# Bidirectional HGRN2 scan beside dense products: where the second key transposes land, how the diagonal score blocks are placed, and how the filler is dealt out at the scan's two ends

## The chip, the core and the metric

The kernel runs on one core of one Trainium2 chip. The metric is the device time of one execution in microseconds (us). TensorE (PE), VectorE (DVE), ScalarE (ACT), GpSimd (POOL) and SyncE (SP) each take their own list of instructions in order and wait for each other by semaphores. PSUM, where TensorE writes, has eight banks of 128 x 512 float32.

## What is computed

One layer of an encoder over 1024 positions of width 1024, in float32. The part around the change is a gated linear recurrence with eight heads of 128, run forwards and backwards, over the projections of the normalised input (shortened):

```python
def _chunk_gated_scan(q, k, v, lf):        # S_t = diag(f_t) S_{t-1} + k_t v_t^T,  o_t = S_t^T q_t
    a = jnp.cumsum(lfb, axis=2)
    decay = jnp.where(tril, jnp.exp(jnp.minimum(a_t - a_s, 0.0)), 0.0)
    scores = jnp.einsum("bhtk,bhsk,bhtsk->bhts", qb, kb, decay)
    o = einsum("bhts,bhsv->bhtv", scores, vb) + einsum("bhtk,bhkv->bhtv", qb * jnp.exp(a), state)
    new_state = jnp.exp(a_last)[..., None] * state + einsum("bhsk,bhsv->bhkv", kb * jnp.exp(a_last - a), vb)

def _token_mixers(h, w_in, ...):
    proj = jnp.einsum("bsd,de->bse", h, w_in)      # conv input, q, v, two forget gates, output gate, two merge gates
    o = _bi_hgrn2(q, v, z_f, z_b, lb[0], lb[1])    # one scan per direction, added
    bmix = rmsnorm_per_head(o) * norm_w * silu(og)
    return sigmoid(g_a) * (a @ pw_w) + sigmoid(g_b) * (bmix @ o_w)
```

Behind it stand an output product, a gated feed-forward block with a short convolution, and a last RMSNorm.

## The kernel before

**Stages.** The kernel projects the normalised input in tiles of 128 columns (first one by one, then in pairs with seven products in place of eight), runs the convolution branch, then the scan, then the products with hgrn_o_w and w_out, then the feed-forward block. The positions are split into two halves of 512. Large products write each float32 operand as a high and a low part and take three matmuls for one (`mm3`, lines 139 to 149: L147, L148 and L149 of the profile).

**The scan** (lines 1026 to 1405) goes over eight heads and, within a head, two halves of 512 positions: sixteen iterations, numbered i = 0 to 15 below. An odd i is a second half. For each one it

- loads q, v and the two gates' inputs (`scan_inputs`, L1067, L1070, L116) and makes the gates on ScalarE (L1071 to L1073);
- builds keys and queries by doubling (`scan_base`, `double_keys`, `double_queries`, L1052), with ScalarE copies of them in another order (L974), and takes score blocks of a width of 32 from them (`level`, L1103), collected in the tile D on VectorE by `copy_predicated` (L1167, L1204);
- takes the wider blocks of 32 and 64 into one bank (`blocks`, L1186), which ScalarE copies to the score tile S (L1214); four more ScalarE copies then place the four diagonal blocks of D into S, one for each group of 32 partitions (L1216);
- turns the keys of both directions with four transposes each (`scan_states`, L1226), which ScalarE copies to kT (L1228), and multiplies them with v for the states (L1235).

One head later `outputs` and `scan_outputs` chain the backward states (L1328), form the outputs from S, v and the states in the one bank of the tag "ob" (L1276), normalise them (L1278, L1281, L510, L511, L1295), turn them back (L1302) and store them gated (L1304, L1308).

**The banks** are dealt out by tag: three "mm", two "sc", two "tr", one "ob" (L97). The dense products accumulate in "mm" banks. Both key transposes, v's transposes (L1376) and the outputs' transposes take "tr" banks.

**The order.** TensorE's list is the program's own order; the lists of the other engines come from a scheduler. What keeps TensorE busy in the scan is `dense`, a stream of 176 pieces of dense products: the last 18 tiles of the input projection, eight pieces each, and the convolution's 1024 columns, four pieces for each of eight tiles. A piece is six matmuls. `Stream.fill(n)` adds n to a debt and executes whole pieces while the debt is at least 1. An iteration has five steps, and after each, `between(FILL)` calls dense.fill(1.82), then one step of the next iteration's base (`ahead.step`), then one step of the previous head's outputs (`pending.fill(1)`). The wait for a score block of 32 stands behind an iteration's first step, that for 64 behind its second.

At the scan's beginning 6 pieces go ahead of the first base, and 3 behind each of its five steps. At its end (lines 1387 to 1401) the last head's outputs are done in steps with pieces in between: `left - 20` comes out negative there, so the debt eats the next pieces, and two are executed ahead of `bm_loads(0)`, eight behind it. `bm_loads` brings the finished heads back for the product with hgrn_o_w, which follows.

A DMA may be issued from SP, from ACT (`nc.scalar.dma_start`) or from POOL; before, ACT issues none. In the built program the DMAs of SP and ACT share eight semaphores in turn, and each waits until the one that had its semaphore last, the eighth before it, has landed.

## Time and profile before

| what | value |
|---|---|
| median of 3 runs | 1783.46 us (1782.06 to 1784.79) |
| the profiled execution | 1786.31 us |
| its span, first to last instruction | 1784.5 us |
| granted TensorE clock, mean | 0.994 |
| the scan with its two ends in the span | about 497 to 917 us |

In a row of the timeline stand the start, the length, the engine, the line, what is written and read, and in brackets the idle time ahead of it with the instruction that ended it. In a row of the waits stand the total, the count and the longest. A row of the windows has the length, then the busy time of each engine with its instructions in brackets, the granted clock, the DMA engines' share and GB/s. A row of the groups ends with busy time, mean ns of one, and the idle time ahead. SPq is SP issuing DMAs.

### The profile page before, as it was taken

The page shows a single profiled execution, that of the slowest core. Times are in us where ns is not written, and L with a number is a line of the kernel's source. Part 1 is how long each engine was busy: PE and PEld are TensorE (multiplying, and loading weights), DVE is VectorE, ACT ScalarE, POOL GpSimd, SP SyncE. Part 2 cuts the span into 40 slices and gives each one's busy share as a digit, 9 for nine tenths or more (in the row PEclk, how much of TensorE's full clock was granted, in tenths as well). Part 3 has the DMA queues.
Part 4 walks back from the last instruction along what each step waited for, and adds up shares of the span by engine and source line. Part 5 has one row for each costly group of instructions (what it writes and reads, how often), then busy time and mean ns, then how long its engine had stood idle before and what let it go on. Part 6 is the DMA issues. An engine that isn't in the chain of part 4 may idle for free.

```text
span 1784.5 us, 30262 instructions
## 1 busy us (share of the span) xinstructions
PE 1733.0 (97%) x11878; PEld 1424.5 (80%) x11878; DVE 1213.2 (68%) x1845; ACT 827.8 (46%) x1582; POOL 152.1 (9%) x165
## 2 busy tenths in 40 slices
PE   8989999999999999999999999999999999999997
PEld 6878877788778888777878887778888888888885
DVE  5599999746678788877446567667667667544455
ACT  7344333234467778776551244344344344422123
POOL 2201111000000000000000002011111111000000
PEclk9999999999999999999999999999999999999998
DMA  8758877756653434435367665667767666534233
GB/s 283 218 151 189 190 179 185 181 162 206 196 183 102 126 120 126 131 103 178 120 216 226 195 201 177 159 146 156 154 143 153 147 147 138 159 103 125 78 91 136
DMA packets 321269, 284.46 MB, mean 159 GB/s; under 512 B 14942, under 2 KB 242022, under 8 KB 321126
## 3 DMA queue, kind: packets, MB, share of 16 engines
q1 hardware_dynamic: 279958, 250.01, 44.9%
q0 software_dynamic: 41168, 32.51, 13.0%
q8 instruction: 93, 1.52, 0.4%
q14 instruction: 50, 0.41, 0.1%
HBM read 189.40 MB, written 76.81 MB: 149 GB/s over the span
## 4 chain that ended last, share of the span: by engine, by line
PE 72%; DMA 10%; DVE 9%; issue 4%; ACT 3%; POOL 1%; SPq 0%; POOLq 0%; ACTq 0%; DVEq 0%
PE mm L147 17%; PE mm L148 17%; PE mm L149 17%; PE sc L147 3%; PE sc L149 3%; PE sc L148 3%; DMA sw<-in_w_in_dram 3%; DVE acc L956 2%; PE ob L1276 2%; DMA wr<-in_w_in_dram 2%; DMA wr<-wr 2%; DVE wp L123 2%; PE tr L147 1%; PE tr L148 1%; PE tr L149 1%
## 5 line engine op out<-in xcount | busy, mean ns | idle before, releaser
L147 PE MATMUL mm<-hx,wp 128*128 128x512 f32 x1144 | 458.5, 401 | 12.5 <-DVE ev L718 7.6
L149 PE MATMUL mm<-hx,wp 128*128 128x512 f32 x1144 | 448.5, 392 | 1.9 <-DVE wp L123 1.9
L148 PE MATMUL mm<-hx,wp 128*128 128x512 f32 x1144 | 447.9, 391 | 0.0
L123 ACT CAST wp<-wr 128x1024 fp32r<-128x1024 f32 (+2 forms) x171 | 162.1, 949 | 339.6 <-PE mm L148 241.9
L147 PEld LDWEIGHTS mm<-hx,wp 128*128 128x128 f32 x1144 | 216.1, 189 | 60.1 <-DVE ev L718 10.6
L149 PEld LDWEIGHTS mm<-hx,wp 128*128 128x128 f32 x1144 | 215.8, 189 | 49.4 <-DVE wp L123 3.2
L148 PEld LDWEIGHTS mm<-hx,wp 128*128 128x128 f32 x1144 | 216.3, 189 | 41.9 <-issue 0.2
L123 DVE TENSOR_TENSOR wp<-wr,wp 128x1024 fp32r<-128x1024 f32 (+2 forms) x169 | 187.0, 1107 | 86.1 <-ACT wp L123 85.5
L956 DVE SCALAR_TENSOR_TENSOR acc<-gl,v_b,acc 128x1024 f32<-128x1024 f32 x120 | 149.5, 1284 | 0.4
L1635 DVE TENSOR_TENSOR xr<-mm,xr 128x512 f32<-128x512 f32 x48 | 33.2, 691 | 72.1 <-PE mm L149 72.1
L367 ACT COPY su<-mm 128x512 f32<-128x512 f32 x82 | 47.5, 579 | 69.2 <-PE mm L149 68.1
L123 ACT CAST wq<-sw 128x1024 fp32r<-128x1024 f32 x41 | 43.0, 1050 | 65.5 <-issue 25.9
L1052 DVE TENSOR_TENSOR kG<-kG,tb 128x512 f32<-128x512 f32 x96 | 65.9, 688 | 5.5 <-PE sc L1186 5.5
L1052 DVE TENSOR_TENSOR qF<-qF,tb 128x512 f32<-128x512 f32 x96 | 65.6, 687 | 4.7 <-ACT A L1084 3.4
L1484 DVE SCALAR_TENSOR_TENSOR tm<-gp,v_a,tm 128x512 f32<-128x512 f32 x88 | 66.0, 750 | 2.0
L147 PE MATMUL mm<-hy,wp 128*128 128x512 f32 x164 | 64.7, 395 | 1.6 <-ACT su L367 1.6
L147 PE MATMUL sc<-hy,wq 128*128 128x512 f32 x164 | 64.6, 394 | 0.0
L148 PE MATMUL mm<-hy,wp 128*128 128x512 f32 x164 | 64.3, 392 | 0.0
L149 PE MATMUL sc<-hy,wq 128*128 128x512 f32 x164 | 64.2, 391 | 0.0
L147 PE MATMUL tr<-hx,wp 128*128 128x512 f32 x164 | 63.9, 390 | 0.0
L149 PE MATMUL tr<-hx,wp 128*128 128x512 f32 x164 | 63.8, 389 | 0.0
L148 PE MATMUL tr<-hx,wp 128*128 128x512 f32 x164 | 63.8, 389 | 0.0
(354 smaller groups left out, 3437.2 us busy)
## 6 DMA issues: line engine op xcount, KB each, us to landing
wr<-in_w_in_dram SPq DMA_DIRECT2D x56, 512.0 KB, 5.0
wr<-in_ffn_w_up_dram SPq DMA_DIRECT2D x24, 512.0 KB, 5.5
sw<-in_ffn_w_up_dram SPq DMA_DIRECT2D x44, 256.0 KB, 4.1
d_g<-ft SPq DMA_DIRECT2D x44, 256.0 KB, 2.5
sw<-in_ffn_w_up_dram POOLq DMA_DIRECT2D x20, 512.0 KB, 8.6
sw<-in_w_in_dram SPq DMA_DIRECT2D x38, 256.0 KB, 3.6
d_z<-ev SPq DMA_DIRECT2D x32, 256.0 KB, 4.6
zi<-d_z SPq DMA_DIRECT2D x32, 256.0 KB, 2.6
```

The lines of the kernel that those rows point to most:

```text
L123: parts = A.copy(hi, src), eng.tensor_tensor(lo, src, hi.bitcast(F32), op=ALU.subtract)
L147: T.matmul(acc, whi[:, k, :], ahi, start=first, stop=False, skip_group_check=again)
L148: T.matmul(acc, whi[:, k, :], alo, start=False, stop=False, skip_group_check=again)
L149: T.matmul(acc, wlo[:, k, :], ahi, start=False, stop=last, skip_group_check=again)
L367: A.copy(t, acc)
L956: V.scalar_tensor_tensor(acc, g[:, k : k + S], tap(k), acc, op0=ALU.mult, op1=ALU.add)
L1052: V.tensor_tensor(o, a, b, op=op)
L1276: T.matmul(o[:, sl], l, r, start=(n == 0), stop=(n == len(terms) - 1))
L1484: V.scalar_tensor_tensor(c, g[:, o + k : o + k + H], vec("fdw", k * NF + j), c, op0=ALU.mult, op1=ALU.add,)
L1635: V.tensor_tensor(xr[i][half], acc, xr[i][half], op=ALU.add)
```

## The change

Three edits. The second direction's key transposes go to a "mm" bank, in the rotation of the dense products. The four ScalarE copies that place the diagonal blocks become four DMAs from D to S issued by ScalarE. The filler is dealt out anew: 7 pieces ahead of the first base and 3, 4, 4, 3, 0 behind its steps (21 as before), 1.77 in place of 1.82 after each step of the scan, and at the end a table of output steps and pieces, with the debt set to zero first.

```diff
-FILL = 1.82
+FILL = 1.77
+TAIL = ((1, 2), (1, 1), (2, 4), (2, 3))
...
         A.copy(S_t, c4(b))
         for g in range(0, P, 32):
-            A.copy(S_t[g : g + 32, :, g : g + 32], D_t[g : g + 32])
+            nc.scalar.dma_start(S_t[g : g + 32, :, g : g + 32], D_t[g : g + 32])
...
-            b = bank("tr")
+            b = bank("mm" if d else "tr")
             for c in range(4):
                 T.transpose(b[:, c * P : (c + 1) * P], kG[:, d, c * P : (c + 1) * P], ident)
...
-    dense.fill(6)
-    for _ in range(5):
+    dense.fill(7)
+    for pieces in (3, 4, 4, 3, 0):
         cur.step(1)
-        dense.fill(3)
+        dense.fill(pieces)
...
-    left = 8 * len(rest) + 4 * ND - dense.count
-    pending.fill(1)
-    dense.fill(left - 20)
-    pending.fill(1)
-    dense.fill(4)
-    pending.fill(2)
-    dense.fill(4)
-    pending.fill(2)
-    dense.fill(4)
+    dense.owed = 0
+    for steps, pieces in TAIL:
+        pending.fill(steps)
+        dense.fill(pieces)
     bm_loads(0)
     pending.fill(1)
-    dense.fill(8)
     dense.drain()
     bm_loads(1)
     pending.drain()
```

## The prediction

> **What bounds the kernel now.** First the page: the span, the busy shares, and the chain that ended last.

> ```profile
> span 1784.5 us, 30262 instructions
> ...
> PE 1733.0 (97%) x11878; PEld 1424.5 (80%) x11878; DVE 1213.2 (68%) x1845; ACT 827.8 (46%) x1582; POOL 152.1 (9%) x165
> ...
> PE 72%; DMA 10%; DVE 9%; issue 4%; ACT 3%; POOL 1%; SPq 0%; POOLq 0%; ACTq 0%; DVEq 0%
> ```

> TensorE is busy for 1733.0 of 1784.5 us and the change takes no matmul away, so it can only win idle time. I read next the windows around the scan: its beginning, its body, its end, two stretches of the end alone, a stretch of dense products, and one of VectorE's fullest.

> ```profile
> 497.60:517.00 19.40, 17.47 (x199) 14.22 (x198) 12.56 (x23) 15.61 (x27) 0.00 (x0) 1.00 0.80 256
> 517.00:886.60 369.60, 358.83 (x5676) 300.20 (x5677) 283.76 (x622) 264.61 (x616) 13.11 (x14) 1.00 0.39 125
> 886.60:916.80 30.20, 26.96 (x143) 22.32 (x141) 10.60 (x20) 17.13 (x45) 1.83 (x2) 0.94 0.47 156
> 900.90:904.30 3.40, 1.47 (x6) 0.93 (x7) 0.88 (x2) 2.41 (x8) 0.96 (x1) 1.00 0.00 0
> 904.30:907.70 3.40, 3.40 (x10) 2.64 (x9) 1.95 (x3) 2.07 (x5) 0.00 (x0) 0.50 0.86 274
> 480.00:500.00 20.00, 20.00 (x90) 16.57 (x89) 7.27 (x10) 6.85 (x10) 0.00 (x0) 1.00 0.56 171
> 729.00:760.00 31.00, 28.66 (x495) 23.53 (x495) 28.19 (x59) 23.13 (x47) 0.00 (x0) 1.00 0.45 137
> ```

> TensorE's idle time is 19.40 - 17.47 = 1.93 us at the beginning, 10.77 in the body, 3.24 at the end. After the end's idle stretch (busy 1.47 of 3.40 us) the granted clock is 0.50 for 3.40 us: half of that, 1.7 us, is lost too. All that can be won is thus 1.9 + 10.8 + 3.2 + 1.7 = 17.6 us. A piece of dense products is six matmuls at 20.00 / 90 us, 1.33 us.

> The waits of TensorE from 500 to 925 us name the places:

> ```profile
> PE sc L1186 <- DVE qF L1052: 4.2, 4, 1.8
> PE tr L1226 <- DVE ev L1304: 3.9, 3, 2.0
> PE tr L1226 <- ACT kT L1228: 2.7, 4, 0.7
> PE tr L1302 <- ACT tm L1295: 2.6, 2, 2.1
> PE sc L1103 <- ACT A L1084: 1.9, 2, 1.6
> PE ob L1276 <- ACT tm L1278: 0.7, 1, 0.7
> ```

> They add up to 16.0 us, the idle time above. The timeline places the first kinds (the longer ones; the four waits for the first transposes' copy are 0.67 each, in the second halves of heads 1, 2, 3 and 5, and 3.9 - 2.05 - 1.45 = 0.4 is left for head 7):

> ```profile
> 599.69 0.69 PE L1186 MATMUL sc<-qF,kG 128*64 128x64 f32 x16 [0.88 <-DVE qF L1052]
> 606.31 0.66 PE L1226 MATMUL tr<-ident,kG 128*128 128x128 f32 x4 [0.68 <-ACT kT L1228]
> 744.84 0.66 PE L1226 MATMUL tr<-ident,kG 128*128 128x128 f32 x4 [2.05 <-DVE ev L1304]
> 755.54 0.46 PE L1186 MATMUL sc<-qF,kG 128*32 128x32 f32 x32 [0.29 <-DVE qF L1052]
> 781.73 0.46 PE L1186 MATMUL sc<-qF,kG 128*32 128x32 f32 x32 [1.83 <-DVE qF L1052]
> 832.44 0.69 PE L1186 MATMUL sc<-qF,kG 128*64 128x64 f32 x16 [1.15 <-DVE qF L1052]
> 839.84 0.66 PE L1226 MATMUL tr<-ident,kG 128*128 128x128 f32 x4 [1.45 <-DVE ev L1304]
> ```

> **The change part by part.**

> **Second key transposes in a "mm" bank.** Every wait at L1226 is for a "tr" bank, held by the first transposes' copy or by an output evacuation. In the changed program these transposes carry no wait but that for their own keys, except in the last iteration, where it is for an eviction long done. All 3.9 + 2.7 = 6.6 us go. The price: a dense half comes round to a bank one turn sooner. A half lasts four pieces, 5.3 us, and its eviction by ScalarE is one copy (L1228, of the same size: 588 ns, below), so I take nothing; without that cover, each of some 35 halves would wait up to 0.6 us.

> What is late next is VectorE: it is busy 28.19 of 31 us around the wait of 2.05. What L1186 needs at 755.5 ends when it ended, however early TensorE comes, so that 2.05 returns there.

> **FILL 1.77.** Whole pieces fall where the sum passes a whole number. Step j gets the whole part of 1.82 j less that of 1.82 (j - 1). So steps 17 (i = 3), 51 (i = 10), 56 (i = 11) and 67 (i = 13) get one piece and not two: the steps ahead of the four waits at L1186 (1, 6, 12 and 62 also get one ahead of an L1186, and none waits). With 1.77, steps 17, 51, 56 and 67 get two; one goes to 27 (i = 5), 31 (i = 6), 57 (i = 11), 61 (i = 12) and 66 (i = 13), ahead of an L1186 too. Over 80 steps it is 141 pieces for 145; four move to the end.

> Together, per head, I weigh the waits removed against the lead that each L1186 had. As an example, i = 12:

> ```profile
> 801.05 1.28 DVE L1052 TENSOR_TENSOR qF<-qF,tb 128x512 f32<-128x512 f32 x2
> 804.18 0.47 PE L1186 MATMUL sc<-qF,kG 128*32 128x32 f32 x32
> ```

> Its lead is 804.18 - 802.33 = 1.85 us; a piece less ahead of it (1.33), a piece less in i = 11 (1.33) and the transposes' 0.67 turn it into a wait of 1.5. In this way I get, for heads 1 to 7, waits of 1.55, 0.67, 0.68, 2.34, 2.50, 2.60 and 0.41 before, and 0, 0.2, 0, 2.3, 1.8, 2.1 and 0 after: 10.75 - 6.4 = **4.3 us** won. Estimates all: VectorE's order is dealt anew by the scheduler. Bounds: nothing, and 10.8.

> **Beginning.** The levels (L1103) stand behind 14 pieces and not 12: 2.7 us more against waits of 1.93, which go. Behind them come two pieces fewer, so L1186 of i = 0 loses about 0.1. **1.8 us** won; bounds 0 and 1.9.

> **End.** The outputs get pieces between them: one ahead of the second half's L1276 (wait 0.7), seven ahead of L1302 where two stood. These rows give what lies between:

> ```profile
> 897.11 0.39 PE L1276 MATMUL ob<-Sf,qF 128*128 128x128 f32 x2
> 902.35 0.33 PE L1302 MATMUL tr<-ident,tm 128*128 128x128 f32 x1 [2.08 <-ACT tm L1295]
> 903.16 0.91 PE L1302 MATMUL tr<-ident,tm 128*128 128x128 f32 x3 [0.48 <-ACT tm L1295]
> ```

> L1302's second transpose starts 903.16 - 897.50 = 5.7 us behind the end of L1276, and seven pieces are 9.3. So 3.2 us of waits go, and with them the half clock's 1.7. Behind the turn stand four pieces, not eight, ahead of the product with hgrn_o_w:

> ```profile
> 916.76 0.48 PE L147 MATMUL mm<-hx,wp 128*128 128x512 f32 x1
> ```

> ```profile
> 918.60 0.68 DVE L123 TENSOR_TENSOR hx<-ev,hx 128x512 fp32r<-128x512 f32 x1
> ```

> Its eighth page, the last head's, was ready at 919.28, and needed 21 matmuls behind 916.76, at 921.4: 2.1 us early. From L1276 to that product there is now one piece more but 4.3 us of idle and half clock less, 3 us in all, so it may be 0.9 late, if nothing ahead of it moves; its chain begins at L1302, which moves too. I take 0.3. **4.6 us** won; bounds 0 and 4.9.

> [...]

> **Diagonal blocks by DMA.** Sixty-four copies leave ScalarE and as many DMA issues join the same places in its list:

> ```profile
> L1216 ACT COPY S<-D 32x128 f32<-32x128 f32 x64 | 18.8, 294 | 1.0
> L1228 ACT COPY kT<-tr 128x512 f32<-128x512 f32 x32 | 18.6, 588 | 5.7 <-PE tr L1226 5.6
> L300 POOL DMA_DIRECT2D sw<-in_w_in_dram x11 | 17.6, 1596 | 82.7 <-DVE wp L123 33.1 <-DMA sw<-in_w_in_dram 23.1 <-DVE su L901 20.5
> ```

> ```profile
> 638.19 3.03 SPq L1070 DMA_DIRECT2D zi<-d_z  x2
> 643.11 0.32 SPq L724 DMA_DIRECT2D d_ga<-ev  x1
> ```

> ```profile
> 630.85 0.59 ACT L1228 COPY kT<-tr 128x512 f32<-128x512 f32 x1
> ...
> 647.70 1.22 ACT L1216 COPY S<-D 32x128 f32<-32x128 f32 x4
> 678.27 0.59 ACT L1228 COPY kT<-tr 128x512 f32<-128x512 f32 x1
> ```

> ```profile
> 633.79 1.06 PE L1235 MATMUL ob<-v,kT 128*128 128x128 f32 x8
> ...
> 679.96 1.06 PE L1235 MATMUL sc<-v,kT 128*128 128x128 f32 x8
> ```

> ScalarE issues no DMA before, so no row has its price. From below it is nothing (the four copies' 1.22 us of ScalarE won), from above POOL's 1.6 us each; I take SP's 0.32, the nearest: 1.28 us for four, no change. Queued behind them are ScalarE's A copies and both kT copies, for which L1235 waits; its shortest lead is 679.96 - 678.86 = 1.1 us, the usual one 633.79 - 631.44 = 2.3. Each issue also waits until the eighth DMA before it has landed; the closest is the second load of zi above, issued by 641.2, which has 6.5 us before the first copy at 647.70. S itself is read a head later. So I take nothing; at POOL's price it would be 16 x (6.4 - 1.22 - 2.3) = 46 us lost, far from the nearest row, and a rival below takes that side.

> [...]

> **Sum:** 1.8 + 4.3 + 4.6 = 10.7 us. The profiled execution is 1786.31 us, 1.8 around its span of 1784.5 and 2.85 above the median of the runs, 1783.46. The span should be 1773.8, and from the median 1783.46 - 10.7 = **1772.8 us**.

> **The rivals.**

> *The scan is bound by VectorE.* The removed 6.6 all come back at L1186; beginning and end alone remain: 6.4 us, 1777.1. For it: 28.19 of 31 busy. Against it: 283.76 of 369.60 in the whole body.

> *Every wait goes.* The scheduler's new order suits; 17.6 us: 1765.9. For it: 86 us of VectorE's body are idle. Against it: the four one-piece steps only move.

> *Issues hold ScalarE.* With x us for each, kT comes 4x - 1.22 later, and L1235 waits for what exceeds 2.3. It eats the 10.7 from x = (10.7 / 16 + 2.3 + 1.22) / 4 = 1.05 us on; at 1.3 it costs 16 x 1.68 = 27 and gives 1783.5 - 10.7 + 27 = 1800. For it: POOL's issues, and SP's x2 row of 3.03, which has waits in it. Against it: SP's 0.32.

> *Edits cancel*: the end's pages come late by what the waits gave, and the body wins nothing: 1782.

> **How the numbers follow.** Forecast 0.55, bound by VectorE 0.2, every wait gone 0.08, cancelled 0.09, ScalarE held 0.08. The range, 1765.5 to 1780.5, covers the first three, 0.83. 0.2% is 3.6 us, about what a measurement of this kernel can tell from no change: faster is below 1779.9, the first three cases, 0.83; same 0.1 with a little of the last two; slower 0.07.

> **What would show it.** L1226 without waits in the waits of TensorE; L1103 without its 1.9; L1302 and L1276 at the end without theirs and no 0.50 clock near 905; L1186 <- DVE about as large as before or larger (4 to 7 us), at i = 10, 12, 13. ScalarE's issues at about 0.3 us, and no wait of L1235 on kT. Wrong would be: waits of dense L147 for "mm" banks, of L1276 for DMAs into S, of L147 for pages of bm behind the turn, or a ScalarE list that runs late.

## The result, and the profile after

| | before | after |
|---|---|---|
| median of 6 runs each, on the same chip | 1783.32 us (1782.06 to 1787.13) | 1775.92 us (1773.77 to 1778.40) |
| span of the profiled execution | 1784.5 us | 1776.6 us |
| from the 2,110th matmul to the 8,201st (the scan with its ends and the turn behind it) | 436.96 us | 428.63 us |

The ratio is 0.9955, with a 95% interval of 0.9941 to 0.9969: 8.0 us faster, between 5.5 and 10.5. The forecast was 10.7.

The third row counts from a matmul to the same matmul of the list, so that both stretches hold the same number of matmuls. It comes from one execution of each kernel. The rest of the span is the same code in every kernel of this document and still varies from 1341 to 1349 us over their fourteen traces (TensorE's long waits near 310, 450 and 1150 us), so the stretch is compared and not the span. It holds the whole of the span's 7.9 us. It is called the scan's time below.

In the changed kernel every line up to the scan's end is numbered one higher than in the kernel before: L1104 are the levels, L1187 the score blocks, L1209 the matmuls that clear their bank, L1217 the placement, L1227 the key transposes, L1236 the state products. The windows of the profile after, as they were shown of before (the beginning, the body, the end):

```profile
497.50:517.00 19.50, 19.50 (x197) 16.06 (x198) 13.57 (x24) 16.50 (x29) 0.00 (x0) 1.00 0.80 262
517.00:879.60 362.60, 354.96 (x5691) 297.57 (x5681) 283.24 (x624) 243.33 (x550) 12.83 (x14) 1.00 0.41 128
879.60:908.00 28.40, 28.23 (x150) 23.66 (x148) 8.46 (x16) 15.93 (x44) 1.83 (x2) 1.00 0.54 169
```

TensorE's idle time is now 0 at the beginning (1.93 before), 362.60 - 354.96 = 7.64 in the body (10.77), 0.17 at the end (3.24), and the clock stays at 1.00 there. The waits of TensorE from 497 to 935 us say what is left:

```profile
PE sc L1187 <- DVE qF L1053: 3.4, 6, 1.0
PE ob L1236 <- ACT kT L1229: 2.1, 2, 1.2
PE ob L1104 <- DVE Sf L1244: 2.0, 5, 0.9
PE mm L150 <- DVE wp L124: 0.7, 2, 0.5
PE mm L148 <- ACT wp L124: 0.2, 1, 0.2
```

The waits of L1226 (6.6 us), L1103 on ScalarE's copies (1.9), L1302 (2.6) and L1276 (0.7) are gone. Three kinds are new: the state products wait for kT, which ScalarE copies; the levels wait for VectorE to free the "ob" bank; and a dense product at the turn waits for weights that VectorE splits. ScalarE's list ahead of the first new wait, and SyncE's beside it (SPq; first rows of two timelines, start and length), show the reason:

```profile
599.13 0.58 ACT L1215 COPY S<-sc 128x512 f32<-128x512 f32 x1
599.74 3.77 ACTq L1217 DMA_DIRECT2D S<-D  x4
603.61 0.62 ACT L1085 COPY A<-qF 128x512 f32<-128x512 f32 x1 [3.89 <-DMA S<-D]
...
606.32 0.60 ACT L1229 COPY kT<-mm 128x512 f32<-128x512 f32 x1
```

```profile
601.36 2.12 SPq L1068 DMA_DIRECT2D q<-d_q  x1
```

```profile
606.48 0.71 PE L1236 MATMUL ob<-v,kT 128*128 128x128 f32 x4 [1.20 <-ACT kT L1229]
```

Four issues hold ScalarE for 3.77 us where the four copies took 1.22, and the copies behind them run as much later. This is the longest of the sixteen groups of four; the shortest take 2.6 us. All 64 issues by their line (min, median and max in ns):

```profile
L1217 ACTq DMA_DIRECT2D S<-D x64: 592/608/1814, 534.6 to 874.7; - x64
```

ScalarE looks less busy after (807.1 us, 827.8 before) only because issues do not count as busy. Not all of their cost is a wait with a name: the levels' matmuls show it as busy time. The group in the profile before, after, and in the first experiment, which has the copies back:

```profile
L1103 PE MATMUL sc<-A,A 128*32 128x32 f32 x1536 | 17.5, 199 | 1.9 <-ACT A L1084 1.9
```

```profile
L1104 PE MATMUL sc<-A,A 128*32 128x32 f32 x1536 | 19.1, 200 | 0.0
```

```profile
L1104 PE MATMUL sc<-A,A 128*32 128x32 f32 x1536 | 17.2, 199 | 0.0
```

The same 1536 matmuls cover 19.1 us and not 17.2: between them lie stalls shorter than the 200 ns that the profile gives a matmul. In the changed kernel 16 of them start 62 to 164 ns behind the one ahead (14 in the middle), in the kernel before none but the two with a wait's row. They read A, and ScalarE's copies of A stand behind the issues. VectorE waits for these copies too: it doubles the queries in place (`qF<-qF,tb`) once ScalarE has copied them to A, and these waits are 14.2 us in all, 3.4 before and 4.0 in the first experiment. The first experiment's list of matmuls is the same, so the two can be compared from start to start. The changed kernel loses 2.6 us at the state products, 1.9 at these levels and 1.7 at the levels in the "ob" bank: 6.2 of the 6.7 us between the two.

### The profile page after: what moved, and what is told of

Same layout as the page of the kernel before. It is cut to its first block, busy times and chain, and to the rows that moved or that the text cites. A ratio compares the mean times of both kernels' runs of the same rounds, so it can differ in the third digit from the quotient of the medians.

```text
span 1776.6 us, 30271 instructions
## 1 busy us (share of the span) xinstructions
PE 1733.0 (98%) x11878; PEld 1424.9 (80%) x11878; DVE 1213.0 (68%) x1845; ACT 807.1 (45%) x1518; POOL 152.0 (9%) x165
## 3 DMA queue, kind: packets, MB, share of 16 engines
q10 hardware_dynamic: 9216, 1.05, 0.4%
## 4 chain that ended last, share of the span: by engine, by line
PE 44%; DMA 5%; issue 2%; ACT 1%; DVE 1%; POOL 0%; SPq 0%; POOLq 0%; ACTq 0%; DVEq 0%
PE mm L148 11%; PE mm L150 11%; PE mm L149 11%; PE sc L148 2%; PE sc L150 2%; PE sc L149 2%; DMA ev<-d_ga 2%; PE tr L149 1%; PE tr L150 1%; PE tr L148 1%; DMA tm<-d_bm 1%; PE ob L1277 1%; DMA sw<-in_ffn_w_up_dram 1%; DMA wr<-wr 0%; DVE tm L1409 0%
## 5 line engine op out<-in xcount | busy, mean ns | idle before, releaser
L1053 DVE TENSOR_TENSOR qF<-qF,tb 128x512 f32<-128x512 f32 x96 | 65.2, 685 | 14.3 <-ACT A L1085 14.2
L1053 DVE TENSOR_TENSOR kG<-kG,tb 128x512 f32<-128x512 f32 x96 | 65.5, 685 | 5.0 <-PE sc L1187 4.6
L148 PE MATMUL sc<-hy,wq 128*128 128x512 f32 x164 | 64.6, 394 | 0.0
L150 PE MATMUL sc<-hy,wq 128*128 128x512 f32 x164 | 64.2, 391 | 0.0
L148 PE MATMUL tr<-hx,wp 128*128 128x512 f32 x164 | 63.9, 390 | 0.0
L150 PE MATMUL tr<-hx,wp 128*128 128x512 f32 x164 | 63.8, 389 | 0.0
L149 PE MATMUL sc<-hy,wq 128*128 128x512 f32 x164 | 63.8, 389 | 0.0
```

The source lines that it names most:

```text
L148: T.matmul(acc, whi[:, k, :], ahi, start=first, stop=False, skip_group_check=again)
L149: T.matmul(acc, whi[:, k, :], alo, start=False, stop=False, skip_group_check=again)
L150: T.matmul(acc, wlo[:, k, :], ahi, start=False, stop=last, skip_group_check=again)
L1053: V.tensor_tensor(o, a, b, op=op)
```

## The experiments

Theory A, from the traces: the transposes in an "mm" bank and the filler win time in the scan, and the placement by DMA gives some of it back, because each issue holds ScalarE for 0.6 us and more. Its rivals were that the DMAs cost nothing and the body is bound by VectorE, or that the DMAs cost by what they move or by landing late. Unless a diff says otherwise, an experiment starts from the changed kernel. The whole set, each timed against the kernel before on its chip:

| experiment | ratio to before (95%) | scan's time, us | against before |
|---|---|---|---|
| the changed kernel | 0.9955 (0.9941 to 0.9969) | 428.63 | -8.3 |
| 1: copies back on ScalarE | 0.9928 (0.9915 to 0.9942) | 421.90 | -15.1 |
| 2: before, mm bank alone | 0.9961 (0.9948 to 0.9973) | 430.15 | -6.8 |
| 3: before, DMAs alone | 1.0047 (1.0034 to 1.0059) | 445.07 | +8.1 |
| 4: before, new ends alone | 0.9992 (0.9983 to 1.0001) | 436.31 | -0.7 |
| 5: issued by GpSimd | 0.9925 (0.9909 to 0.9940) | 422.31 | -14.7 |
| 6: issued by SyncE | 0.9936 (0.9918 to 0.9954) | 423.53 | -13.4 |
| 7: eight issues for four | 1.0108 (1.0090 to 1.0126) | 457.99 | +21.0 |
| 8: as 1, with 1.82 | 0.9964 (0.9953 to 0.9976) | 430.16 | -6.8 |
| 9: as 1, both transposes in tr | 0.9987 (0.9976 to 0.9997) | 432.81 | -4.2 |
| 10: copies on GpSimd | 0.9925 (0.9908 to 0.9942) | 421.48 | -15.5 |
| 11: as 5, filler from a table | 0.9927 (0.9909 to 0.9945) | 422.66 | -14.3 |

Scan's time, from one trace each, and timed ratio agree to some 2 us in every row; the intervals are 1.6 to 3.2 us to each side.

### 1. Copies back on ScalarE

```diff
-            nc.scalar.dma_start(S_t[g : g + 32, :, g : g + 32], D_t[g : g + 32])
+            A.copy(S_t[g : g + 32, :, g : g + 32], D_t[g : g + 32])
```

> The changed kernel with the four ScalarE copies from D to S back in place of the DMAs; the other two edits stay. Theory A (the issues cost time): in the changed kernel four issues hold ScalarE for 2.6 to 3.8 us where the four copies took 1.2, and both waits of the state products (L1236) on kT, 2.1 us, come from that; here they go, and VectorE's wait for ScalarE's A copies shrinks: 2 to 4 us faster than the changed kernel, a ratio to before of 0.9932 to 0.9944. Rival B (the placement by DMA is free or helps): ScalarE's copies come back, no wait of TensorE goes: 0.9955 or above, and L1236 waits about as long as with the DMAs.

Median 1771.09 us, 4.8 below the changed kernel by the ratios and 6.7 by the scan's time. The waits of TensorE from 497 to 935 us:

```profile
PE sc L1187 <- DVE qF L1053: 3.3, 7, 1.0
PE mm L150 <- DVE wp L124: 1.1, 2, 0.5
PE ob L1104 <- DVE Sf L1244: 0.3, 1, 0.3
PE mm L148 <- ACT wp L124: 0.2, 1, 0.2
```

The waits for kT (2.1) go, those for Sf fall from 2.0 to 0.3, and the levels' group is back at 17.2. The score blocks' waits for VectorE stay (3.4 to 3.3). The DMAs cost, somewhat more than either theory had.

### 2. The mm bank alone

The kernel before, with:

```diff
-            b = bank("tr")
+            b = bank("mm" if d else "tr")
```

> The kernel before with the second key transposes in a mm bank, nothing else. Theory A (waits move in part): the 6.6 us at the transposes' line go, two to four of them come back at the score blocks (DVE qF) and at other lines that wait for VectorE; 2.5 to 4.5 us faster, ratio 0.9975 to 0.9986. Rival B (the body is bound by VectorE): all of it comes back, ratio 0.9992 to 1.0005. Rival C: nothing comes back, 6.6 us, ratio 0.9963.

Median 1776.76 us, close to rival C's ratio (0.9961 for 0.9963). All waits at L1226 are gone; these are left:

```profile
PE sc L1186 <- DVE qF L1052: 5.3, 4, 1.8
PE tr L1302 <- ACT tm L1295: 2.6, 2, 2.1
PE sc L1103 <- ACT A L1084: 1.1, 1, 1.1
PE ob L1276 <- ACT tm L1278: 0.7, 1, 0.7
```

Only 5.3 - 4.2 = 1.1 us come back at the score blocks, at one place:

```profile
749.76 0.24 PE L1186 MATMUL sc<-qF,kG 128*32 128x32 f32 x4 [1.44 <-DVE qF L1052]
```

It was 0.29 before (at 755.54), behind the largest wait that went (2.05). The body's idle time falls by 6.6 - 1.1 = 5.5 us; 0.8 more go at the beginning (1.9 to 1.1), which the edit does not touch. Against that, the clock at the end is at half for 6.8 us and not 3.4, behind the same wait of 2.1 (893.8 to 900.6), another 1.7 us lost: 4.6 in all, where the scan's time shows 6.8.

Most of the difference lies in how a wait is shown. Its row counts the idle time from the modelled end of the matmul ahead. In the kernel before, the dense product behind one pair of transposes starts 1.69 us after the first transpose (605.04 to 606.73), here 0.80 (602.98 to 603.78): the wait's row says 0.68, and 0.89 are won. Taken so, the seven waits were worth 8.1 us and not 6.6. Rival C's number came out although 1.1 us did come back.

### 3. The DMAs alone

The kernel before, with:

```diff
-            A.copy(S_t[g : g + 32, :, g : g + 32], D_t[g : g + 32])
+            nc.scalar.dma_start(S_t[g : g + 32, :, g : g + 32], D_t[g : g + 32])
```

> The kernel before with the diagonal blocks placed by DMA, nothing else. Theory A: each issue holds ScalarE 0.6 us and more where SP issues at the same time; the state products wait for kT, and the copies for the levels run late: 1 to 4 us slower, ratio 1.0005 to 1.0022. Rival B: no change or faster, ratio 0.998 to 1.0003, with no wait for kT.

Median 1792.33 us: 8.8 slower, over twice theory A's upper end. The first two waits, and two windows of the body:

```profile
PE tr L1226 <- ACT kT L1228: 6.0, 4, 2.5
PE sc L1186 <- DVE qF L1052: 4.1, 4, 1.8
```

```profile
702.50:705.90 3.40, 3.40 (x14) 3.02 (x13) 2.24 (x7) 3.10 (x6) 0.00 (x0) 0.50 0.56 205
750.30:753.70 3.40, 3.40 (x11) 2.72 (x10) 3.35 (x11) 2.98 (x6) 0.00 (x0) 0.50 0.68 235
```

With both transposes in "tr" banks, a late kT holds a bank, and the next transposes wait: 2.7 us became 6.0. Behind two waits of this line the clock was granted at half for 3.4 us each, another 3.4 us lost: behind one of 2.49 us for kT, and behind one of 1.70 us for VectorE's `ev`. The second stands in the kernel before too, with 2.05 us and no half clock (the last section has both), so this part of the loss is not the DMAs' work alone. Neither happened in the changed kernel, where the second transposes have an "mm" bank: there the DMAs cost 6.7 us of the scan's time, here 8.1.

### 4. The new ends alone

The kernel before, with the new beginning and the table at the end; 1.82, the copies and the tr banks stay.

> The kernel before with the new dealing at the beginning (7 and 3, 4, 4, 3, 0) and at the end (the table, the debt set to zero), with 1.82 kept, the transposes in the tr banks and the copies on ScalarE. Theory A: idle time of 1.9 us at the beginning and of 3.2 + 1.7 at the end goes, and up to 1.5 us come back behind the turn, where weights and pages come late: 4.5 to 6.5 us faster, ratio 0.9963 to 0.9975, the body's 10.8 us unchanged. Rival B: the end's gain is all lost to late pages and weights: about 2 us, ratio 0.9985 to 0.9995.

Median 1782.53 us: 1.4 us faster by the ratio, with an interval that reaches no change. All the idle time of beginning and end goes, as expected, and comes back behind the turn:

```profile
PE mm L148 <- ACT hx L124: 2.3, 1, 2.3
PE mm L150 <- DVE wp L124: 0.5, 1, 0.5
PE mm L149 <- DVE hx L124: 0.5, 2, 0.3
```

```profile
911.50:913.20 1.70, 0.04 (x1) 0.00 (x0) 0.00 (x0) 0.05 (x1) 0.00 (x0) 1.00 0.97 369
913.20:920.00 6.80, 6.17 (x14) 4.63 (x15) 4.61 (x8) 4.19 (x7) 0.00 (x0) 0.50 0.74 252
```

The product with hgrn_o_w waits 2.3 us for a page of the last head, and the clock is at half for 6.8 us. With 1.82 nothing stands behind the turn: 176 pieces less 21, 145 and the table's 10 leave 0; with 1.77 they leave 4. Rival B's kind of loss, here with its reason.

### 5 and 6. Another engine issues

```diff
-            nc.scalar.dma_start(S_t[g : g + 32, :, g : g + 32], D_t[g : g + 32])
+            nc.gpsimd.dma_start(S_t[g : g + 32, :, g : g + 32], D_t[g : g + 32])
```

and, in the sixth, `nc.sync.dma_start`.

> The changed kernel with the four DMAs from D to S issued by GpSimd in place of ScalarE. Theory A (what costs is that the issues hold ScalarE): ScalarE has neither copies nor issues, so it is at least as fast as with the copies: ratio to before 0.9915 to 0.9935, no wait of the state products for kT. Rival B (the transfers themselves cost, by landing late or by disturbing other transfers): as with ScalarE's issues, 0.9948 to 0.9962. Rival C: the issues hold up GpSimd's own small steps in the normalisation of the outputs, and the outputs' transposes wait: above 0.9948 with waits of L1303 for ScalarE's tm.

> The changed kernel with the four DMAs issued by SyncE in place of ScalarE. Theory A (the issue's length belongs to the shape of the transfer, and the cost to the engine that issues): SyncE's issues of these take 0.6 us each as ScalarE's did, against 0.32 for its loads of whole pages; ScalarE is free, 0.9915 to 0.9940. Rival B (ScalarE is slow at issuing): SyncE's take 0.3 to 0.4 us. Rival C: the loads of q and the gates stand behind the issues' wait for D in SyncE's list and land late: above 0.995.

Medians 1769.13 and 1771.51 us. The same 64 transfers, from the same line, by GpSimd and by SyncE:

```profile
L1217 POOL DMA_DIRECT2D S<-D x64: 549/552/634, 533.4 to 867.0; - x64
```

```profile
L1217 SPq DMA_DIRECT2D S<-D x64: 591/597/1421, 532.7 to 868.2; - x64
```

The transfers run as before, and the time is that of the copies, with no wait of the state products for kT: it is the hold on ScalarE that costs, not the transfers (the fifth's rival B). SyncE needs 0.6 us for each as ScalarE does, so between these two the length belongs to the transfer and not to the engine (against the sixth's rival B). Neither rival C shows: no transpose waits for `tm`, and the sixth is not above 0.995. Its interval, though, overlaps that of the changed kernel; its gain is clear by the scan's time alone, where it is 5.1 us. GpSimd, busy for 12.83 us of the body, has time for the issues.

### 7. Eight issues for four

```diff
-            nc.scalar.dma_start(S_t[g : g + 32, :, g : g + 32], D_t[g : g + 32])
+            for h2 in (0, 2):
+                nc.scalar.dma_start(
+                    S_t[g : g + 32, h2 : h2 + 2, g : g + 32], D_t[g : g + 32, h2 : h2 + 2]
+                )
```

> The changed kernel with eight DMAs of half the size in place of each four, issued by ScalarE. Theory A (each issue holds ScalarE some 0.6 us whatever its size): 4.9 us and more per half in place of 2.7; 16 halves by 2.2 us are 35 us of ScalarE, of which a quarter to all shows: 8 to 35 us slower than the changed kernel, ratio 1.000 to 1.015. Rival B (the length goes with the rows moved, or the hold costs nothing): as the changed kernel, 0.9945 to 0.9965.

Median 1802.79 us, 27 above the changed kernel. The issues by their line, and the first waits of TensorE:

```profile
L1218 ACTq DMA_DIRECT2D S<-D x128: 592/607/1812, 531.1 to 901.7; - x128
```

```profile
PE ob L1239 <- ACT kT L1232: 11.0, 10, 2.8
PE sc L1187 <- DVE qF L1053: 9.5, 8, 1.8
PE ob L1104 <- DVE Sf L1247: 6.1, 4, 1.9
```

Half the pieces, 0.607 us where it was 0.608. 64 more issues are 39 us of ScalarE, and the time grows by 27. Of these 27, 6.8 go to the clock, which was at half for 6.8, 3.4 and 3.4 us (from 753.5, 815.0 and 842.3). All three kinds of waits grow, those for VectorE too: its doubling of the queries waits 48.3 us for ScalarE's copies to A, 14.2 with four issues.

### 8. The filler's number

The first experiment's kernel with `FILL = 1.82`.

> The first experiment's kernel (copies on ScalarE) with 1.82 in place of 1.77 after each step; transposes in mm banks, the new beginning and end. Theory A (four pieces more at the end are what covers the turn, and the steps ahead of the score blocks get their piece): 4 to 7 us slower than with 1.77, ratio 0.9950 to 0.9967, with a wait for the last heads' pages behind the turn and 5 us of waits at the score blocks. Rival B (the number matters little): 0.9920 to 0.9940.

Median 1777.34 us, 6.4 slower than with 1.77 by the ratios. The first two waits:

```profile
PE sc L1187 <- DVE qF L1053: 5.3, 4, 1.8
PE mm L148 <- ACT hx L124: 2.6, 1, 2.6
```

The clock is at half twice, behind the wait of 1.84 us at a score block and behind the 2.6 at the turn:

```profile
773.90:777.30 3.40, 3.40 (x42) 2.86 (x33) 3.40 (x7) 2.30 (x5) 0.00 (x0) 0.50 0.32 101
910.40:913.80 3.40, 3.40 (x10) 2.62 (x9) 2.62 (x5) 2.38 (x4) 0.00 (x0) 0.50 0.66 201
```

1.77 takes 5.3 - 3.3 = 2.0 us of waits and 1.7 of half clock from the score blocks, and somewhat more from the turn, as in the fourth. The scan's time equals that of the mm bank alone (430.16, 430.15): without 1.77 the new ends are worth nothing.

### 9. Both transposes in tr banks

The first experiment's kernel with `bank("tr")`: of the change, the filler alone.

> The first experiment's kernel (copies on ScalarE, 1.77, the new ends) with the second key transposes back in a tr bank. Theory A (this edit's 6.6 us of waits are its own and hardly come back elsewhere, with the new filler as without it): the waits at the transposes' line return, 5 to 7 us slower than with the mm bank, ratio to before 0.9956 to 0.9970. Rival B (the filler's new dealing would have moved the waits anyway): 0 to 3 us slower, 0.9926 to 0.9945.

Median 1781.49 us, 10.5 slower than with the mm bank. The first three waits:

```profile
PE tr L1227 <- DVE ev L1305: 6.7, 4, 2.8
PE sc L1187 <- DVE qF L1053: 2.8, 5, 1.0
PE tr L1227 <- ACT kT L1229: 2.0, 3, 0.7
```

Theory A was right in kind and low in size: with the new filler the waits at the transposes are 8.7 us, not 6.6, and behind one of 2.34 us the clock is at half:

```profile
739.70:743.10 3.40, 3.40 (x11) 2.81 (x12) 3.40 (x9) 2.35 (x5) 0.00 (x0) 0.50 0.97 287
```

By the scan's time the two edits help each other: -6.8 and -4.2 alone, -15.1 together. By the ratios it is -7.0, -2.3 and -12.8, and the 3.5 us that the pair wins beyond the sum are no larger than the noise of three such intervals.

### 10. Copies on GpSimd

```diff
-            nc.scalar.dma_start(S_t[g : g + 32, :, g : g + 32], D_t[g : g + 32])
+            nc.gpsimd.tensor_copy(S_t[g : g + 32, :, g : g + 32], D_t[g : g + 32])
```

> The changed kernel with four copies by GpSimd from D to S in place of the four DMAs. Theory A (any engine that has time will do, ScalarE's list is what counts): as with GpSimd's issues, 0.9915 to 0.9935. Rival B (GpSimd's copies slow VectorE's instructions that run beside them): VectorE's mean times at L1053 rise above 685 ns and the waits of the score blocks for it above 4 us: 0.994 or more.

Median 1771.13 us, the same as GpSimd's issues. VectorE's instructions at L1053 keep their means (690 and 686 ns for the two largest groups, 685 and 686 with GpSimd's issues), so these were slowed by 5 ns at most, and the waits of the score blocks for VectorE are 3.8 us, below rival B's 4.

### 11. The filler from a table

```diff
+    deals = iter([n for i in range(NI) for n in ((2, 2, 2, 1, 1) if i in (4, 9, 14) else (2, 2, 2, 2, 1))])
...
-                between(FILL)
+                between(next(deals))
```

in both places, on the fifth experiment's kernel.

> GpSimd's issues with the 141 pieces of the body dealt by a table: two behind each of an iteration's first three steps, one behind the last, and 2, 2, 2, 1, 1 in iterations 4, 9 and 14, so that no score block has a single piece ahead of it. Theory A (what is left at the score blocks, 3.5 us in 7 waits, is the steps with a single piece ahead): the waits at i = 5, 11 and 13, 0.6, 0.6 and 1.0 us, go, and 1 to 2.5 us in all: ratio 0.9908 to 0.9920. Rival B (VectorE's work sets these times, and a piece more here is waited for elsewhere): no change, 0.9920 to 0.9935, with 3 us or more of waits for VectorE in the body.

Median 1770.63 us, no change. The first two waits of TensorE:

```profile
PE ob L1104 <- DVE Sf L1244: 4.4, 5, 1.2
PE mm L150 <- DVE wp L124: 0.5, 1, 0.5
```

All seven waits at the score blocks went, as theory A had it, and the time did not, as rival B had it: 4.4 us of waits for VectorE stand at the levels instead. In both dealings what is left of the body's waits is for VectorE.

### 12. What an issue costs

One execution of the first experiment's kernel with four more DMAs per half whose data nobody reads; only the lengths of its issues are used:

```diff
+        nc.sync.dma_start(whole, D_t)
+        nc.sync.dma_start(part[:32], D_t[:32])
+        nc.sync.dma_start(d_dd[0][0][:, :P], D_t.rearrange("p c e -> p (c e)"))
+        nc.scalar.dma_start(d_dd[0][1], qF[:, 0, :])
```

> A price list, not a contender: the first experiment's kernel (copies on ScalarE) with four more DMAs per half whose data nobody reads: D to another tile of SBUF over all 128 partitions, D's first 32 partitions to another tile (both issued by SyncE), D to DRAM (SyncE), and a page of 128 x 512 to DRAM issued by ScalarE. Theory A (an issue from SBUF to SBUF takes 0.6 us whatever its partitions, one to or from DRAM 0.32, on either engine): 0.6, 0.6, 0.32 and 0.32 us. Rival B (blocks of 32 partitions cost 0.6): 0.32, 0.6, 0.32, 0.32. Rival C (ScalarE takes twice as long as SyncE): the last is 0.6.

```profile
L1220 SPq DMA_DIRECT2D whole<-D x16: 478/479/1662, 529.7 to 862.1; - x16
L1222 SPq DMA_DIRECT2D part<-D x16: 556/591/988, 530.3 to 862.7; - x16
L1223 SPq DMA_DIRECT2D d_dd<-D x16: 425/573/1397, 530.9 to 863.9; - x16
L1224 ACTq DMA_DIRECT2D d_dd<-qF x16: 326/326/350, 535.3 to 869.4; - x16
```

Rival C falls: ScalarE issues a whole page to DRAM in 0.326 us, as SyncE does. Theory A and rival B each hold only in part: 128 partitions from SBUF to SBUF take 0.48 us, 32 partitions 0.59, and the small store to DRAM 0.43 at least (0.57 in the middle). The price goes with the shape; by which rule stays open.

## Why the prediction came out as it did

The sign and the range held, and so did the mechanisms of the transposes, the beginning and the end. The step on the DMAs did not, and the body's gain was mis-sized the other way; that the two nearly cancelled was luck. Of the prediction's own signs, issues of 0.3 us and no wait on kT failed, and "a ScalarE list that runs late", which it named as a sign of being wrong, came.

- **Second key transposes: mis-sized.** "All 3.9 + 2.7 = 6.6 us go" held to the letter, with no wait of the dense halves for a bank; from start to start it was 8.1 (experiment 2). The step "that 2.05 returns there" did not hold: 1.15 of it came back, and nothing of the other waits.
- **Body, 4.3 us: mis-sized.** The body's idle time fell by 3.1 with the DMAs, and in the first experiment, without them, by 10.77 - 3.74 = 7.0. The likeliest case was thought out for this kernel with ScalarE on time, and left 6.4 us of waits at the score blocks, nearly all in heads 4 to 6. With ScalarE on time 3.3 were left, half of them in heads 1 and 2. (Its list of steps with one piece leaves out step 22, in i = 4; no wait stands behind it.) The body in the first experiment:

```profile
517.00:872.10 355.10, 351.36 (x5656) 295.23 (x5655) 280.24 (x618) 260.19 (x612) 13.10 (x14) 1.00 0.39 127
```

- **Beginning, 1.8 us: right.** 1.93 of idle time went.
- **End, 4.6 us: right.** 3.24 - 0.17 = 3.1 of idle time and 1.7 of half clock went, 0.5 came back at the turn at a dense product that waits for weights, where 0.3 for late pages was taken: 4.3. What the step left unsaid is that all of it hangs on the four pieces that 1.77 moves there (experiments 4 and 8).
- **Diagonal blocks by DMA, nothing: wrong.** The step that failed is "I take SP's 0.32, the nearest". The row is a fair price for a page of 256 KB to or from DRAM (ScalarE takes 0.326 us for one, experiment 12), but these are four blocks of 16 KB within SBUF. They took 0.608 us, four together 2.6 us undisturbed and up to 3.77, not 1.28. It cost 4.8 us by the ratios and 6.7 by the scan's time.
- **The rival "issues hold ScalarE": right in kind, its length too long and its rule too mild.** It took 1.3 us for an issue. At the measured 0.61 us its rule, 4x - 1.22 against a lead of 2.3, gives no loss, and 0.25 us at 3.77 for four; the trace has waits of 1.20 and 0.85 for kT, 1.7 more for Sf, and 1.9 in the levels' group. The rule looked at kT alone. The A copies stand behind the issues too, VectorE waits for these, and the levels and the "ob" bank wait for both.
- **Issues of two engines at once: open.** With SyncE's issue beside them, the longest of ScalarE's lasted 1.81 us and SyncE's 2.12. But in the kernel before, where ScalarE issues nothing, 11 of SyncE's 191 issues from 497 to 917 us lasted 0.78 to 2.16, and in the sixth, where ScalarE issues nothing either, its issues of these blocks took 0.60 in the middle and 1.42 at most. In the changed kernel 28 of ScalarE's 64 issues had one of SyncE's beside them, and 23 of these took no more than 0.70. What makes a few issues long stays open; the 0.6 us of the others are no wait for an issue of SyncE's, since the 36 without one beside them took 0.59 to 0.80.
- **The rival "bound by VectorE": half right.** Of the 6.6 only 1.1 came back, but what was left then was waits for VectorE, in both dealings of the filler (experiment 11).

So the scan won 15.1 us by the other two edits. TensorE's waits fell from 16.0 to 4.9 us, the half clock's 1.7 went, and the seven waits at the transposes were worth 1.5 more than their rows say: 11.1 + 1.7 + 1.5 = 14.3; the rest was not traced. The DMAs took 6.7 back. The 10.7 forecast came within 3 us of the 8.0 measured because a gain and a loss that were both left out largely cancelled.

The first experiment's kernel, and its three variants with GpSimd or SyncE, beat the changed kernel and the one before: 11.4 to 13.4 us faster than before, not to be told apart by these runs.

## What to carry to other kernels

Price a DMA issue by a row with the same kind of transfer, not with the same engine, and count it against the list of the engine that issues it: "busy" does not show it, and replacing a 0.3 us copy by a 0.6 us issue was a loss on ScalarE, for which others wait. Put such work on the engine with the emptiest list; here GpSimd took it for nothing. When filler is moved, ask first how many pieces are left for the place with the longest chain, here the turn behind the scan, and measure edits in pairs: the new ends won nothing with 1.82, and with 1.77 they won 4.2 us of the scan's time together (1.77 without the new ends was not run). Do not read a gain off the rows of the waits alone: add the half clock behind them, and about 0.2 us for each wait here.

## What the runs showed of the hardware

The time of an issue did not fall with its pieces: 0.608 us with 32 rows of four pieces, 0.607 with two (experiment 7). It did change with the shape: 0.48 us for 128 rows (experiment 12).

```profile
740.45:743.86 3.41, 2.34 (x137) 2.06 (x136) 3.41 (x7) 2.66 (x7) 0.00 (x0) 1.00 0.90 282
743.86:747.28 3.42, 2.44 (x13) 2.12 (x14) 3.42 (x9) 2.26 (x6) 0.00 (x0) 1.00 0.64 210
```

The shorter one of 1.70 in experiment 3 was followed by half clock from 750.30. A wait of 2.77 us in experiment 9 (ended at 601.36) brought none; counted back from the half clock at 739.70, the grid cuts it at 599.75, into 1.16 and 1.61. Where the grid lies against the program differs from trace to trace: its first line is 3.19 us behind the span's start in the kernel before, 1.53 in the changed one. So whether a wait of about 2 us cost another 1.7 us (3.4 us at half clock) or none was chance in these runs.
